# Norm 1 by column scale: chunks of a transposed input, and the tokens' inverse norms applied to the mixer's products

## The chip, the core and the metric

The kernel runs on one core of a Trainium2 chip. The core's engines work side by side, each through its own list of instructions: TensorE (PE, with its weight loads as PEld), VectorE (DVE), ScalarE (ACT), GpSimd (POOL), and SyncE (SP), which here issues nearly all DMAs. The metric is device time in microseconds of one execution.

## The reference, cut to what matters

```python
h = rms_norm(x, norm1)                   # x * rsqrt(mean(x*x) + EPS) * norm1, 2048 tokens of 1024
p = h @ w_in
lru_x, lru_g, q, k, v, g, z = split(p)
lru_x = causal_depthwise_conv(lru_x)     # then two gates and a scan over the sequence
lru_o = rg_lru(lru_x) * gelu(lru_g)
log_alpha = log_sigmoid(z @ gla_w_alpha + gla_b_alpha) / 16
o = gla_chunk_causal(q / 8, k, v, log_alpha)
gla_o = rms_norm(o, gla_norm) * silu(g)
x = x + concat(lru_o, gla_o) @ w_out
x = x + ffn(rms_norm(x, norm2))          # SwiGLU, 1024 -> 2 x 2816 -> 1024
return rms_norm(x, final_norm)
```

All is float32. The norm's inverse root is one number for each token, norm1 one for each column of `x`.

## The kernel before, in words

The 2048 tokens are worked in four blocks of 512 (`b` = 0 to 3), and in a block in four tiles of 128 (`t`). Each large product is three matmuls (`mm3`, L248 to L250): both operands are split into a high part (a cast on ACT) and a low part (a subtraction on DVE), which `split` does at L258 and `split_scaled` with a column scale at L283 and L284. A part of `h`, the normed input, is needed with its 128 columns on the partitions and the 512 tokens along the rows, and there are eight such chunks in a block.

`Norm1` makes them. It loads the block's four tiles of `x` (tokens on partitions), sums their squares on ACT (`sumsq`, L219), takes the inverse roots on DVE (`rsqrt`, eleven small instructions, L231 to L240, from `rv` to `rs`), scales the tiles on DVE (L310), and transposes them chunk by chunk on PE (L320 in the first block, L329 later).

`mixer(b)` then runs, on PE in this order: the products for k and z (L562 reads them), four products for the conv channels, each followed by the conv on ACT and DVE (`lru_conv`), the products for v with the eight gate products between them (`lru_gates`), two products for q (`feat(h)`, read at L641), the state updates (L654), the output half of the block before or, in block 0, `lru_out`, and so on. Behind the last gate stands a chain on two other engines: ACT takes a root (L622) and an exponential (L625), and DVE runs the four scans of the channel groups (`lru_scan`, L525 to L529; the scan itself is L527). In the program's text the next block's `Norm1` is made behind these scans, and its transposes are spread over `lru_out`.

The order of instructions on each engine is not that of the text: a scheduler sets it when the program is built, by its own estimate of times. What an engine has been given it works off in that order. Buffers in the arena are handed out by hand; a load into a reused place waits until the last reader is done, and everything behind it on SP waits too. PSUM has eight banks (`mm`).

Of the kernel before, what the change touches and what calls it, by code (L numbers as in the profile page):

```python
# [15 lines left out]
P = 128  # L16
# [162 lines left out]
def hybrid_layer_kernel(  # L179
    ctx: ExitStack,  # L180
    tc: tile.TileContext,
    x: bass.AP,
    wf: bass.AP,
    wkz: bass.AP,
    wv: bass.AP,
# [28 lines left out]
    def small(n, name):  # L214
        return cp.tile([P, n], F32, tag=f"s{n}", name=name, bufs=10 if n < 16 else 6)
# [81 lines left out]


    class Norm1:
        def __init__(self, b, group=TT):  # L300
            self.xs = [load(x_v[b * TT + t], D) for t in range(TT)]
            for g in range(0, TT, group):
                ss = small(group, "ss")
                for i in range(group):
                    sumsq(ss[:, i : i + 1], self.xs[g + i].f(D), D)
                rs = small(group, "rs")
                rsqrt(rs, [ss], 1.0 / D, group)
                for i in range(group):
                    v = self.xs[g + i].f(D)
                    nc.vector.tensor_scalar(v, v, rs[:, i : i + 1], None, op0=ALU.mult)  # L310
            self.h = []

        def half(self, g):
            if g == 0:
                self.h = [pair(T, True) for _ in range(KC)]
            for c in range(KC):
                ps = bank()
                for i in range(2):
                    v = self.xs[2 * g + i].f(D)
                    nc.tensor.transpose(ps[:, i * P : (i + 1) * P], v[:, c * P : (c + 1) * P], ident)  # L320
                split_scaled(self.h[c], ps[:, : 2 * P], cc(C_N1 + c), slice(2 * g * P, (2 * g + 2) * P))
            if g == 1:
                A.free(*self.xs)

        def chunk(self):
            c = len(self.h)
            ps = bank()
            for t in range(TT):
                nc.tensor.transpose(ps[:, t * P : (t + 1) * P], self.xs[t].f(D)[:, c * P : (c + 1) * P], ident)  # L329
            b = pair(T, True)  # L330
            split_scaled(b, ps, cc(C_N1 + c), slice(0, T))
            self.h.append(b)
            if c == KC - 1:
                A.free(*self.xs)


    class Feed:
# [53 lines left out]
    feed = Units(all_units, 2)  # L391

    wal_b, zta_b = A.alloc(256), A.alloc(T)
    nxt = Norm1(0, 2)
    nc.sync.dma_start(ident, ident_in)
    nc.sync.dma_start(col, cols)
    feed.ahead = 4
    feed.fill()
    feed.ahead = 2

    sfx = cp.tile([P, P], F32, name="sfx")
    nc.sync.dma_start(sfx, sfx_in)
# [71 lines left out]
    def tokmaj_first(norm, n):  # L474

        pss = [bank() for _ in range(TT)]
        wbs = [feed.get() for _ in range(4)]
        for g in range(2):
            norm.half(g)
            for c in range(KC):  # L480
                wh, wl = wbs[c // 2][c % 2].r(n)
                mh, ml = norm.h[c].r(T)
                for t in (2 * g, 2 * g + 1):
                    s = slice(t * P, (t + 1) * P)
                    mm3(pss[t][:, :n], mh[:, s], ml[:, s], wh, wl, c == 0, c == KC - 1)
        for wb in wbs:
            A.free(*wb)
        return pss

    def lru_conv(b, f, ps):  # L490
        buf = A.alloc(T)
        xc = buf.f(T)
        nc.scalar.activation(xc, ps, AF.Identity, scale=cc(C_CW + 12 + f), bias=cc(C_CB + f))
        hl = cp.tile([P, 3], F32, tag="halo", name="halo", bufs=8)
        nc.vector.tensor_copy(hl, ps[:, T - 3 : T])
        for s in (1, 2, 3):
            w = cc(C_CW + (3 - s) * 4 + f)
            nc.vector.scalar_tensor_tensor(xc[:, s:], ps[:, : T - s], w, xc[:, s:], op0=ALU.mult, op1=ALU.add)
            if b > 0:
                nc.vector.scalar_tensor_tensor(  # L500
                    xc[:, :s], halo[f][:, 3 - s : 3], w, xc[:, :s], op0=ALU.mult, op1=ALU.add
                )
        halo[f] = hl
        return buf

    def lru_gates(f, xcb):
# [47 lines left out]
    def mixer(b, norm, prev, side):  # L554
# [4 lines left out]
        pss = tokmaj_first(norm, 272) if b == 0 else tokmaj(norm.h, 272, [lambda: run(side, 1)] * 4)  # L559
        h = norm.h  # L560
        for t, ps in enumerate(pss):
            nc.scalar.copy(kz[:, t, :], ps[:, :272])  # L562
        xcs = [lru_conv(b, 0, feat(h))]
        run(side, 2)
        zps = bank()
        for t in range(TT):
            nc.tensor.transpose(zps[:16, t * P : (t + 1) * P], kz[:, t, 256:272], ident)
        nc.vector.tensor_copy(zta[:16, :], zps[:16, :])
        xcs.append(lru_conv(b, 1, feat(h)))
        run(side, 2)  # L570
        zfs = []
        for t2 in range(2):
# [13 lines left out]
                nc.scalar.activation(las[t2].f(), las[t2].f(), AF.Ln, bias=1.0)  # L586
        for t2 in range(2):
            nc.vector.scalar_tensor_tensor(las[t2].f(), zfs[t2], 0.0, las[t2].f(), op0=ALU.min, op1=ALU.subtract)
        xcs.append(lru_conv(b, 2, feat(h)))
        run(side)  # L590
        xcs.append(lru_conv(b, 3, feat(h)))
        dps = bank()
        dview = dps[:, :16].rearrange("p (a n) -> p a n", a=2)
        eks = []
# [29 lines left out]
            for f in range(4):  # L624
                nc.scalar.activation(gts[f][0].f(), gts[f][0].f(), AF.Exp, scale=sc_a[:, f : f + 1])  # L625
        vs = []
        for ps in vps:
            v = A.alloc(T)
            nc.scalar.copy(v.f(), ps)
            vs.append(v)  # L630
        hs = [lru_scan(b, f, gts[f]) for f in range(4)]
        after = None
        if b + 1 < NB:
            after = Norm1(b + 1)


        qs = []
        for a in range(2):
            ps = feat(h)
            q = A.alloc(T)  # L640
            nc.scalar.activation(q.f(), ps, AF.Copy, scale=0.125)  # L641
            qs.append(q)
        state = stc[(b + 1) % 2]
        sts = []
# [35 lines left out]
        def lru_out():  # L680
            for f in range(4):
                ps = feat(h)
                g = A.alloc(T)
                nc.scalar.activation(g.f(), ps, AF.Gelu_apprx_tanh)
                nc.vector.tensor_mul(g.f(), g.f(), hs[f].f())
                mixt[f] = split(g.f(), T)
                A.free(g, hs[f])
                if after is not None:
                    for _ in range((0, 2, 3, 3)[f] if b == 0 else 2):
                        after.chunk()  # L690
# [44 lines left out]

        for t, ps in enumerate(tokmaj(h, T)):
            sg = A.alloc(T)
            nc.scalar.activation(sg.f(), ps, AF.Silu)
# [8 lines left out]

        if b > 0:
            lru_out()
        A.free(*h)  # L750
        for hd in range(4):
            ps = bank()
            for t in range(TT):
# [627 lines left out]
def _layout(i):  # L1381
    import numpy as np

    f = {k: np.asarray(v) for k, v in i.items()}
    w_in = f["w_in"][0]
    c = np.ascontiguousarray

    def featu(w):
        k, m = w.shape
        return c(w.reshape(k // P, P, m // P, P).transpose(2, 1, 0, 3)).reshape(m // P, P, k)  # L1390

    def toku(w):
# [24 lines left out]
    ind = np.where(t[:, None] // 64 == np.arange(2)[None, :], 1.0 / 16.0, 0.0)  # L1417
    return {
        "x": c(f["x"][0]), "wf": wf, "wkz": wkz, "wv": wv, "wg": wg, "wo": wo, "wgu": wgu, "w2": w2,
        "cols": c(cols), "wgate": c(wgate), "walpha": c(walpha), "fnorm": c(f["final_norm"]),  # L1420
        "ident": np.eye(P, dtype=np.float32), "sfx": sfx.astype(np.float32), "ind": ind.astype(np.float32),
    }
# [19 lines left out]
```

## Time and profile before

| | |
|---|---|
| median of 3 runs | 2057.82 us (2056.31 to 2059.64) |
| profiled execution | 2056.9 us, of it span 2055.1 us |
| PE busy | 2004.1 us, 98% of the span |
| DVE, ACT busy | 1335.3 us (65%), 884.0 us (43%) |
| TensorE clock granted, mean | 0.991 |

The mixer blocks take about the first 750 us of the span, the feed-forward part the rest. A busy PE is one with a matmul under way, so the 51 us in which it is not busy are the waits that a change can take away, and what is shorter or gone in its matmuls comes beside them. A wait is read by its releaser: the instruction, on another engine, whose end let the waiting one start.

### The profile page before, as it was taken

How to read it: one execution, taken by the hardware profiler on the slowest of the kernel's cores; microseconds unless marked ns; L12 is line 12 of the kernel's file. 1: busy time of each engine (PE TensorE's matmuls, PEld its weight loads, DVE VectorE, ACT ScalarE, POOL GpSimd, SP SyncE). 2: the span in 40 equal slices, each digit the busy share in tenths (PEclk: the TensorE clock that was granted, in tenths of full speed). 3: DMA queues.
4: the chain of work that ended last, by engine and by line, in shares of the span. 5: the costliest groups of instructions: out<-in, count | busy, mean ns of one | idle time of the engine just before them, and what ended most of it. 6: DMA issues, size and time to landing. Idle time of an engine off the chain costs nothing.

```text
span 2055.1 us, 26677 instructions
## 1 busy us (share of the span) xinstructions
PE 2004.1 (98%) x9520; PEld 1652.2 (80%) x9520; DVE 1335.3 (65%) x2390; ACT 884.0 (43%) x1523; POOL 178.0 (9%) x216
## 2 busy tenths in 40 slices
PE   7999999999999999999999999999999999999997
PEld 6878788878878878888888887888888788888876
DVE  5575656575555586666777777777775555656676
ACT  5655635654553454443444554444443212212332
POOL 0000000000000000000011001111120222222110
PEclk9999999999999999999999999999999999999999
DMA  5142245243524653567467656577576955755642
GB/s 184 44 153 72 90 147 191 77 141 126 170 69 153 204 180 113 169 199 221 159 217 228 191 152 218 193 219 236 195 235 221 354 164 177 242 170 159 227 131 82
DMA packets 211174, 353.21 MB, mean 172 GB/s; under 512 B 19409, under 2 KB 95458, under 8 KB 211042
## 3 DMA queue, kind: packets, MB, share of 16 engines
q1 hardware_dynamic: 196898, 304.32, 46.1%
q0 software_dynamic: 14144, 47.20, 6.1%
q8 instruction: 74, 1.21, 0.3%
q14 instruction: 58, 0.48, 0.1%
HBM read 244.49 MB, written 106.95 MB: 171 GB/s over the span
## 4 chain that ended last, share of the span: by engine, by line
PE 89%; DVE 4%; ACT 2%; DMA 2%; issue 1%; POOL 0%; DVEq 0%; SPq 0%; POOLq 0%; ACTq 0%
PE mm L248 29%; PE mm L249 29%; PE mm L250 29%; DMA arena_r<-w2c 1%; DVE arena L527 1%; PE mm L858 1%; DMA arena_r<-ad 1%; DVE arena L525 0%; DVE arena L526 0%; PE mm L329 0%; ACT arena L622 0%; PE mm L600 0%; PE mm L710 0%; PE mm L576 0%; DVE arena_r L258 0%
## 5 line engine op out<-in xcount | busy, mean ns | idle before, releaser
L249 PE MATMUL mm<-arena_r 128*128 128x512 f32 (+1 forms) x2596 | 1004.6, 387 | 9.4 <-DVE carry L529 8.0
L250 PE MATMUL mm<-arena_r 128*128 128x512 f32 (+1 forms) x2584 | 998.3, 388 | 0.9 <-DVE arena_r L258 0.9
L248 PE MATMUL mm<-arena_r 128*128 128x512 f32 (+1 forms) x2512 | 980.2, 391 | 9.0 <-DVE arena L1199 8.0
L249 PEld LDWEIGHTS mm<-arena_r 128*128 128x128 f32 x2596 | 489.9, 189 | 104.7 <-DVE carry L529 8.9
L248 PEld LDWEIGHTS mm<-arena_r 128*128 128x128 f32 x2512 | 473.3, 189 | 121.8 <-DVE arena L1199 13.6
L250 PEld LDWEIGHTS mm<-arena_r 128*128 128x128 f32 x2584 | 487.9, 189 | 100.7 <-DVE arena_r L258 1.3
L258 ACT CAST arena_r<-arena 128x512 fp32r<-128x512 f32 (+1 forms) x465 | 277.3, 612 | 461.5 <-PE mm L249 241.2
L258 DVE TENSOR_TENSOR arena_r<-arena,arena_r 128x512 fp32r<-128x512 f32 (+1 forms) x464 | 308.9, 677 | 217.8 <-ACT arena_r L258 204.1
L1199 DVE TENSOR_TENSOR arena<-arena,mm 128x512 f32<-128x512 f32 x272 | 186.3, 686 | 142.6 <-PE mm L250 142.5
L1165 ACT CAST arena_r<-arena_r 128x896 fp32r<-128x896 f32 (+1 forms) x88 | 80.1, 915 | 288.2 <-PE mm L249 184.5
L1070 POOL DMA_DIRECT2D w2c<-arena x127 | 68.7, 541 | 770.8 <-DMA ad<-arena 376.8
L1166 POOL TENSOR_TENSOR arena_r<-arena_r 128x896 fp32r<-128x896 f32 x40 | 85.4, 2136 | 320.4 <-PE mm L250 125.9
L258 ACT CAST arena_r<-swing 128x512 fp32r<-128x512 f32 x90 | 55.8, 621 | 106.8 <-PE mm L249 37.3
L219 ACT ACTIVATE arena<-arena 128x512 bf16<-128x512 f32 (+1 forms) x64 | 46.9, 733 | 81.8 <-DVE arena L1199 26.0
L258 ACT CAST swing<-arena 128x512 fp32r<-128x512 f32 (+1 forms) x83 | 48.1, 593 | 70.2 <-PE mm L250 30.3
L258 DVE TENSOR_TENSOR arena_r<-swing,arena_r 128x512 fp32r<-128x512 f32 x90 | 61.7, 687 | 22.9 <-ACT arena_r L258 18.7
L249 PE MATMUL mm<-arena_r,swing 128*128 128x512 f32 x164 | 65.3, 398 | 4.2 <-DVE arena_r L258 4.2
L959 ACT COPY arena<-mm 128x512 f32<-128x512 f32 x100 | 58.4, 584 | 22.8 <-PE mm L250 21.9
L248 PE MATMUL mm<-swing,arena_r 128*128 128x512 f32 (+1 forms) x164 | 60.5, 369 | 3.8 <-DVE arena_r L284 2.2
L248 PE MATMUL mm<-arena_r,swing 128*128 128x512 f32 x156 | 62.5, 402 | 0.0
L982 DVE TENSOR_TENSOR arena<-mm,arena 128x512 f32<-128x512 f32 x43 | 29.7, 691 | 50.3 <-PE mm L250 50.3
L250 PE MATMUL mm<-swing,arena_r 128*128 128x512 f32 (+1 forms) x168 | 61.2, 365 | 0.0
(210 smaller groups left out, 1650.3 us busy)
## 6 DMA issues: line engine op xcount, KB each, us to landing
arena_r<-w2c SPq DMA_DIRECT2D x148, 256.0 KB, 5.3
arena<-in_wgu_dram SPq DMA_DIRECT2D x142, 256.0 KB, 3.8
arena_r<-ad SPq DMA_DIRECT2D x80, 448.0 KB, 3.5
w2c<-arena POOLq DMA_DIRECT2D x127, 256.0 KB, 3.6
ad<-arena SPq DMA_DIRECT2D x122, 256.0 KB, 3.2
arena<-in_wf_dram SPq DMA_DIRECT2D x40, 512.0 KB, 3.5
arena<-in_wo_dram SPq DMA_DIRECT2D x32, 512.0 KB, 3.9
arena<-in_w_dram SPq DMA_DIRECT2D x41, 256.0 KB, 4.4
```

What stands on the lines that cost most here:

```text
L219: nc.scalar.activation(b.ap.bitcast(BF16), src, AF.Square, accum_out=dst)
L248: nc.tensor.matmul(ps, lhsT=sh, rhs=mh, start=first, stop=False, skip_group_check=again)
L249: nc.tensor.matmul(ps, lhsT=sh, rhs=ml, start=False, stop=False, skip_group_check=again)
L250: nc.tensor.matmul(ps, lhsT=sl, rhs=mh, start=False, stop=last, skip_group_check=again)
L258: b.ins = [nc.scalar.copy(hi, src).ins, nc.vector.tensor_sub(lo, src, hi.bitcast(F32)).ins]
L527: nc.vector.tensor_tensor_scan(m, a, u, 0.0 if b == 0 else carry[f], op0=ALU.mult, op1=ALU.add)
L959: nc.scalar.copy(b.f(), ps[:, :n])
L982: nc.vector.tensor_mul(u1.f(), pa[:, :n], u1.f())
L1070: nc.gpsimd.dma_start(w2c[k][:, m, i * T : (i + 1) * T], part.f())
L1165: nc.scalar.copy(hi, v)
L1166: (nc.gpsimd if i == 1 else nc.vector).tensor_tensor(lo, v, hi.bitcast(F32), op=ALU.subtract)
L1199: nc.vector.tensor_add(c, c, ps)
```

## The change

`x` comes a second time, laid out as `xt` with columns on partitions, chunk by chunk. `Norm1.chunk` now loads a chunk of `xt` and splits it with the column scale norm1; there are no transposes and no scaled tiles. The split parts lack the tokens' inverse norms, so everything made from them is scaled afterwards: products with tokens on partitions by the column `rs` (in the ACT instruction that reads them: k and z, v, the silu gate), products with tokens along the rows by a tile `rb`, which holds the inverse norms along the row, alike on all partitions (on DVE: the conv's input, q, the gelu gate). `scales` makes both: it still loads the four tiles of `x`, sums squares and takes roots, then widens each of the four columns to 128 equal columns on DVE and multiplies them with the identity on PE, and ACT copies the bank to `rb`.

```diff
     class Norm1:
+        def __init__(self, b):
+            self.b = b
             self.h = []
+            self.raws = []
+        def fetch(self):
+            c = len(self.h) + len(self.raws)
+            if c < KC:
+                self.raws.append(load(xt[self.b, c], T))
         def chunk(self):
             c = len(self.h)
-            ps = bank()
-            for t in range(TT):
-                nc.tensor.transpose(ps[:, t * P : (t + 1) * P], self.xs[t].f(D)[:, c * P : (c + 1) * P], ident)
+            raw = self.raws.pop(0)
             b = pair(T, True)
-            split_scaled(b, ps, cc(C_N1 + c), slice(0, T))
+            split_scaled(b, raw.f(), cc(C_N1 + c), slice(0, T))
+            A.free(raw)
             self.h.append(b)
+            self.fetch()
+        def scales(self):
+            ss = small(TT, "ss")
+            xs = [load(x_v[self.b * TT + t], D) for t in range(TT)]
+            for t in range(TT):
+                sumsq(ss[:, t : t + 1], xs[t].f(D), D)
+            A.free(*xs)
+            self.rs = cp.tile([P, TT], F32, tag="rs1", name="rs1", bufs=2)
+            rsqrt(self.rs, [ss], 1.0 / D, TT)
+            wide = A.alloc(T)
+            ps = bank()
+            for t in range(TT):
+                w = wide.f(TT, P)[:, t, :]
+                nc.vector.tensor_copy(w, self.rs[:, t : t + 1].to_broadcast([P, P]))
+                nc.tensor.matmul(ps[:, t * P : (t + 1) * P], lhsT=w, rhs=ident, start=True, stop=True)
+            A.free(wide)
+            self.rb = A.alloc(T)
+            nc.scalar.copy(self.rb.f(), ps)
...
-    def lru_conv(b, f, ps):
+    def lru_conv(b, f, ps, rb):
+        raw = A.alloc(T)
+        nc.vector.tensor_mul(raw.f(), ps, rb)
+        ps = raw.f()
...
-            nc.scalar.copy(kz[:, t, :], ps[:, :272])
+            nc.scalar.activation(kz[:, t, :], ps[:, :272], AF.Copy, scale=norm.rs[:, t : t + 1])
...
             after = Norm1(b + 1)
+            after.fetch()
+            after.fetch()
+            after.scales()
...
-            nc.scalar.activation(q.f(), ps, AF.Copy, scale=0.125)
+            nc.vector.scalar_tensor_tensor(q.f(), ps, 0.125, rb, op0=ALU.mult, op1=ALU.mult)
...
-                nc.scalar.activation(g.f(), ps, AF.Gelu_apprx_tanh)
+                nc.vector.tensor_mul(g.f(), ps, rb)
+                nc.scalar.activation(g.f(), g.f(), AF.Gelu_apprx_tanh)
```

In block 0 the k and z products are no longer made in two halves of the tokens: `tokmaj_first` splits two chunks, multiplies them for all four tiles, and so on, and calls `scales` at its end. In the blocks behind it `scales` is called right behind the text of the scans, as above. What the scheduler makes of it shows in three places.

On PE in block 0, at the end of the v products: before, the last gate product (bank 763) is followed by the first product for q (bank 839).

```order
L248 MATMUL mm_763<-arena_r_64 128x512
L249 MATMUL mm_763<-arena_r_64 128x512
L250 MATMUL mm_763<-arena_r_64 128x512
L248 MATMUL mm_839<-arena_r_64 128x512
L249 MATMUL mm_839<-arena_r_64 128x512
```

Now, with the last gate product in bank 701 and q's first in bank 785, `scales` of block 1 (L336) stands between them.

```order
L249 MATMUL mm_701<-arena_r_64 128x512
L250 MATMUL mm_701<-arena_r_64 128x512
L251 MATMUL mm_701<-arena_r_64 128x512
L336 MATMUL mm_770<-ident_67,arena_63 128x128 x4
L249 MATMUL mm_785<-arena_r_64,swing_65 128x512
L250 MATMUL mm_785<-arena_r_64,swing_65 128x512
```

The four products of the inverse norms have been put in ahead of q and of the state updates; blocks 1 and 2 have them in the same place.

On DVE in block 0, around the four scans: before, two low parts of weights (L258) and the state updates' sums (L669) come behind the scans (L525 to L529), and only then the roots (`rv`).

```order
L525 SCALAR_TENSOR_TENSOR arena<-arena 128x512
L526 TENSOR_TENSOR arena<-arena 128x512 x2
L527 SCALAR_TENSOR_TENSOR arena<-arena 128x512 x2
L529 COPY carry<-arena 128x1
L258 TENSOR_TENSOR arena_r<-arena,arena_r 128x512
L529 COPY carry<-arena 128x1
L258 TENSOR_TENSOR arena_r<-arena,swing 128x512
L669 SCALAR_TENSOR_TENSOR arena<-stc_169,dec,mm 128x128 x2
L669 SCALAR_TENSOR_TENSOR arena<-arena,dec,mm 128x128 x5
L231 TENSOR_SCALAR rv<-ss 128x4
```

Now the scans (L540 to L544) are followed by three low parts of chunks (L285) and the roots; behind the piece shown come seven more of the small instructions and the four copies (L335) that the products at L336 take.

```order
L540 SCALAR_TENSOR_TENSOR arena<-arena 128x512
L541 TENSOR_TENSOR arena<-arena 128x512 x2
L542 SCALAR_TENSOR_TENSOR arena<-arena 128x512 x2
L544 COPY carry<-arena 128x1
L285 SCALAR_TENSOR_TENSOR arena_r<-arena,col,arena_r 128x512
L544 COPY carry<-arena 128x1
L285 SCALAR_TENSOR_TENSOR arena_r<-arena,col,arena_r 128x512 x2
L232 TENSOR_SCALAR rv<-ss 128x4
L236 TENSOR_SCALAR ry<-rv 128x4
L239 SCALAR_TENSOR_TENSOR rt<-ry 128x4
L240 TENSOR_TENSOR rt<-rt,rv 128x4
L259 TENSOR_TENSOR arena_r<-arena,arena_r 128x512
```

The roots have moved ahead of the state updates' sums, but stay behind all four scans.

On SP at the start: before, the four tiles of `x` are the first loads.

```order
L272 DMA arena<-in_x_dram 128x1024 x4
L395 DMA ident<-in_ident_dram 128x128
L396 DMA col<-in_cols_dram 128x49
L272 DMA arena<-in_wkz_dram 128x544 x4
L272 DMA arena<-in_wf_dram 128x1024
```

Now they are the 25th to 28th transfer. Ahead of the piece shown stand the column constants, three chunks of `xt` and two weights of the k and z products; the piece begins with the small constants.

```order
L408 DMA ident<-in_ident_dram 128x128
L411 DMA sfx<-in_sfx_dram 128x128
L413 DMA ind<-in_ind_dram 128x2
L415 DMA arena<-in_walpha_dram 17x256
L422 DMA arena<-in_wgate_dram 64x4x64 x4
L273 DMA arena<-in_xt_dram 128x512 x2
L273 DMA arena<-in_wkz_dram 128x544 x2
L273 DMA arena<-in_xt_dram 128x512 x2
L273 DMA arena<-in_wf_dram 128x1024
L273 DMA arena<-in_xt_dram 128x512
L273 DMA arena<-in_wf_dram 128x1024 x2
L273 DMA arena<-in_x_dram 128x1024 x4
```

The `x` tiles, on which only `scales` depends, have moved from the head of the queue to behind all chunks, all weights of k and z, and three of the conv's weights (`wf`).

## Rows read from the trace of the kernel before

**Rows 1.** The page: span, and busy time (share) and count of each engine.

```profile
span 2055.1 us, 26677 instructions
PE 2004.1 (98%) x9520; PEld 1652.2 (80%) x9520; DVE 1335.3 (65%) x2390; ACT 884.0 (43%) x1523; POOL 178.0 (9%) x216
```

**Rows 2.** PE's waits, whole span: releaser, us in total, times, longest.

```profile
PE mm L320 <- DVE arena L310: 9.8, 1, 9.8
PE mm L249 <- DVE carry L529: 8.0, 2, 4.1
...
PE mm L249 <- DVE arena_r L258: 5.6, 2, 4.2
...
PE mm L329 <- DVE arena L310: 1.0, 3, 0.3
```

**Rows 3.** Groups by form, 0 to 760 us: count | busy us, mean ns | idle before.

```profile
L329 PE MATMUL mm<-ident,arena 128*128 128x128 f32 x96 | 12.9, 274 | 1.4 <-DVE arena L310 1.0 <-PE mm L250 0.5
...
L545 DVE TENSOR_TENSOR arena<-arena,mm 128x512 f32<-128x512 f32 x32 | 20.2, 682 | 3.5 <-PE mm L250 3.5
...
L310 DVE TENSOR_SCALAR arena<-arena,rs 128x1024 f32<-128x1024 f32 x16 | 11.4, 768 | 0.1
```

**Rows 4.** The chain that ended last: start us, us, pieces (L576 has 256 columns).

```profile
45.29 1.92 PE mm L576 x8
...
122.91 1.31 PE mm L329 x12
```

**Rows 5.** Timeline of PE at five places: start us, us, instruction, idle before.

```profile
33.78 0.40 PE L248 MATMUL mm<-arena_r 128*128 128x512 f32 x1
...
88.93 0.39 PE L248 MATMUL mm<-arena_r 128*128 128x512 f32 x1
...
224.79 0.39 PE L248 MATMUL mm<-arena_r,swing 128*128 128x512 f32 x1
...
242.59 0.80 PE L249 MATMUL mm<-arena_r,swing 128*128 128x512 f32 x1 [4.20 <-DVE arena_r L258]
...
410.75 0.39 PE L248 MATMUL mm<-arena_r,swing 128*128 128x512 f32 x1
```

**Rows 6.** Timeline of DVE behind the gates of blocks 0, 1 and 2.

```profile
103.21 2.33 DVE L527 TENSOR_TENSOR_SCAN arena<-arena 128x512 f32<-128x512 f32 x2
...
109.35 0.17 DVE L231 TENSOR_SCALAR rv<-ss 128x4 f32<-128x4 f32 x1 [0.17 <-ACT arena L219]
...
232.15 1.29 DVE L525 SCALAR_TENSOR_TENSOR arena<-arena 128x512 f32<-128x512 f32 x2 [5.52 <-ACT arena L625]
...
239.44 2.46 DVE L527 TENSOR_TENSOR_SCAN arena<-arena,carry 128x512 f32<-128x512 f32 x2
...
249.88 0.17 DVE L231 TENSOR_SCALAR rv<-ss 128x4 f32<-128x4 f32 x1 [1.94 <-ACT arena L219]
250.09 0.17 DVE L235 TENSOR_SCALAR ry<-rv 128x4 int32<-128x4 int32 x1
...
425.34 2.46 DVE L527 TENSOR_TENSOR_SCAN arena<-arena,carry 128x512 f32<-128x512 f32 x2
...
435.45 0.17 DVE L231 TENSOR_SCALAR rv<-ss 128x4 f32<-128x4 f32 x1 [1.61 <-ACT arena L219]
```

**Rows 7.** Timeline of ACT in block 1: the first sum of squares.

```profile
244.46 1.06 ACT L219 ACTIVATE arena<-arena 128x1024 bf16<-128x1024 f32 x1 [8.54 <-DMA arena<-in_x_dram]
```

**Rows 8.** Loads of x, 0 to 130 us: from issue to landing.

```profile
DMA to landing us min/median/max: 3.5/4.9/6.2
```

**Rows 9.** Busy us by stretch: PE, PEld, DVE, ACT, POOL; PEclk, DMA share, GB/s.

```profile
4.00:12.00 8.00, 2.04 (x9) 1.65 (x10) 4.71 (x21) 7.05 (x16) 1.18 (x2) 1.00 1.04 403
...
242.00:249.00 7.00, 6.41 (x16) 5.05 (x17) 5.94 (x20) 4.23 (x8) 0.40 (x1) 0.53 0.87 304
...
300.00:350.00 50.00, 49.97 (x283) 43.53 (x282) 29.64 (x58) 24.76 (x48) 0.00 (x0) 1.00 0.52 171
...
429.50:433.00 3.50, 3.50 (x10) 2.71 (x9) 3.50 (x15) 1.33 (x3) 0.00 (x0) 0.51 0.94 365
```

More of the change, by code (lines that the diff above doesn't have):

```diff
@@ L182, in hybrid_layer_kernel @@
     x: bass.AP,
+    xt: bass.AP,
     wf: bass.AP,
@@ L299, in hybrid_layer_kernel @@
     class Norm1:
[L300 to L310, printed above, removed]
-            self.h = []
@@ L313, in half @@
[L313 to L316, printed above, removed]
-                ps = bank()
[L318 to L323, printed above, removed]
+        def __init__(self, b):
+            self.b = b
+            self.h = []
+            self.raws = []
@@ L325, in chunk @@
+        def fetch(self):
+            c = len(self.h) + len(self.raws)
+            if c < KC:
+                self.raws.append(load(xt[self.b, c], T))
         def chunk(self):
             c = len(self.h)
+            raw = self.raws.pop(0)
+            b = pair(T, True)
+            split_scaled(b, raw.f(), cc(C_N1 + c), slice(0, T))
+            A.free(raw)
+            self.h.append(b)
+            self.fetch()
[8 more added lines that the diff above has]
+            wide = A.alloc(T)
@@ L327, in chunk @@
             ps = bank()
             for t in range(TT):
-                nc.tensor.transpose(ps[:, t * P : (t + 1) * P], self.xs[t].f(D)[:, c * P : (c + 1) * P], ident)
-            b = pair(T, True)
-            split_scaled(b, ps, cc(C_N1 + c), slice(0, T))
-            self.h.append(b)
-            if c == KC - 1:
-                A.free(*self.xs)
+                w = wide.f(TT, P)[:, t, :]
+                nc.vector.tensor_copy(w, self.rs[:, t : t + 1].to_broadcast([P, P]))
+                nc.tensor.matmul(ps[:, t * P : (t + 1) * P], lhsT=w, rhs=ident, start=True, stop=True)
@@ L393, in hybrid_layer_kernel @@
     wal_b, zta_b = A.alloc(256), A.alloc(T)
-    nxt = Norm1(0, 2)
-    nc.sync.dma_start(ident, ident_in)
     nc.sync.dma_start(col, cols)
-    feed.ahead = 4
+    nxt = Norm1(0)
+    nxt.fetch()
+    feed.fetch()
+    nxt.fetch()
+    nxt.fetch()
+    feed.ahead = 1
     feed.fill()
     feed.ahead = 2
+    nc.sync.dma_start(ident, ident_in)
     sfx = cp.tile([P, P], F32, name="sfx")
@@ L476, in tokmaj_first @@
         pss = [bank() for _ in range(TT)]
[L477 to L481, printed above, removed]
+        for kp in range(4):
+            for _ in range(2):
+                norm.chunk()
+            wb = feed.get()
+            for i in range(2):
+                wh, wl = wb[i].r(n)
+                c = 2 * kp + i
                 mh, ml = norm.h[c].r(T)
-                for t in (2 * g, 2 * g + 1):
+                for t in range(TT):
                     s = slice(t * P, (t + 1) * P)
                     mm3(pss[t][:, :n], mh[:, s], ml[:, s], wh, wl, c == 0, c == KC - 1)
-        for wb in wbs:
             A.free(*wb)
+        norm.scales()
         return pss
-    def lru_conv(b, f, ps):
+    def lru_conv(b, f, ps, rb):
+        raw = A.alloc(T)
+        nc.vector.tensor_mul(raw.f(), ps, rb)
+        ps = raw.f()
         buf = A.alloc(T)
@@ L503, in lru_conv @@
         halo[f] = hl
+        A.free(raw)
         return buf
@@ L561, in mixer @@
         for t, ps in enumerate(pss):
-            nc.scalar.copy(kz[:, t, :], ps[:, :272])
-        xcs = [lru_conv(b, 0, feat(h))]
+            nc.scalar.activation(kz[:, t, :], ps[:, :272], AF.Copy, scale=norm.rs[:, t : t + 1])
+        rb = norm.rb.f()
+        xcs = [lru_conv(b, 0, feat(h), rb)]
         run(side, 2)
@@ L568, in mixer @@
         nc.vector.tensor_copy(zta[:16, :], zps[:16, :])
-        xcs.append(lru_conv(b, 1, feat(h)))
+        xcs.append(lru_conv(b, 1, feat(h), rb))
         run(side, 2)
@@ L588, in mixer @@
             nc.vector.scalar_tensor_tensor(las[t2].f(), zfs[t2], 0.0, las[t2].f(), op0=ALU.min, op1=ALU.subtract)
-        xcs.append(lru_conv(b, 2, feat(h)))
+        xcs.append(lru_conv(b, 2, feat(h), rb))
         run(side)
-        xcs.append(lru_conv(b, 3, feat(h)))
+        xcs.append(lru_conv(b, 3, feat(h), rb))
         dps = bank()
@@ L626, in mixer @@
         vs = []
-        for ps in vps:
+        for t, ps in enumerate(vps):
             v = A.alloc(T)
-            nc.scalar.copy(v.f(), ps)
+            nc.scalar.activation(v.f(), ps, AF.Copy, scale=norm.rs[:, t : t + 1])
             vs.append(v)
@@ L737, in mixer @@
             sg = A.alloc(T)
-            nc.scalar.activation(sg.f(), ps, AF.Silu)
+            nc.scalar.activation(sg.f(), ps, AF.Silu, scale=norm.rs[:, t : t + 1])
             sgv = sg.f(2, 2, P)
@@ L749, in mixer @@
             lru_out()
-        A.free(*h)
+        A.free(*h, norm.rb)
         for hd in range(4):
@@ L1418, in _layout @@
     return {
-        "x": c(f["x"][0]), "wf": wf, "wkz": wkz, "wv": wv, "wg": wg, "wo": wo, "wgu": wgu, "w2": w2,
+        "x": c(f["x"][0]), "xt": c(f["x"][0].reshape(NB, T, KC, P).transpose(0, 2, 3, 1)), "wf": wf, "wkz": wkz, "wv": wv, "wg": wg, "wo": wo, "wgu": wgu, "w2": w2,
         "cols": c(cols), "wgate": c(wgate), "walpha": c(walpha), "fnorm": c(f["final_norm"]),
```

## The prediction

> **What bounds the kernel now.** I read the page first: PE is busy for 2004.1 of 2055.1 us [rows 1], so the time is PE's work plus about 51 us of waits. The list of PE's waits says where they are [rows 2]: 9.8 us at the start, until the first tiles of x are scaled, and waits of some 4 us each in the blocks. The timeline of PE places the one of block 1 at 242.59, 4.20 us [rows 5]. The timeline of DVE shows why: the scans run until 241.90 (239.44 + 2.46), and the low part of a weight stands behind them [rows 6]. So the scans are already the place where PE runs out of work: behind the last gate DVE first idles 5.52 us for ACT's root and exponential, then starts the scans at 232.15 [rows 6]. Before, PE had something to do in that time: q's products from 224.79 on [rows 5] and the state updates. The reader should keep this gap in mind, because the change puts something into it.
>
> **The transposes that go.** In blocks 1 to 3, 96 transposes (L329) take 12.9 us at most, with the overlap to their neighbours counted in [rows 3]. Twelve in a row take 1.31 us in the chain, 0.109 each [rows 4]: 96 x 0.109 = 10.5 us. I take the chain's value, since matmuls overlap; 12.9 is the other end. Their three short waits for L310 go too, 1.0 us [rows 2].
>
> The Trainium skill (TensorE: Matmul & The Clock Gate, Part 4: PE-mode transpose) gives about 275 ns for a 128x128 transpose inside a kernel. The row's mean of one, 274 ns [rows 3], looks the same, but the chain shows that they follow each other at 0.109 us. By the page 26.4 us would be saved and the sum below would be 15.9 us less.
>
> **The products that come.** Each `scales` adds four f32 products of 128 columns. The trace has none; the nearest row is L576, f32 with 256 columns, where four products are eight records in 1.92 us, 0.24 a record [rows 4]. At half the columns 0.12, so 12 products for blocks 1 to 3 are 24 x 0.12 = 2.9 us (between 1.9 and 5.8: a fixed cost as large as the whole, or none). The four of block 0 are in the start below.
>
> **The wait that comes.** In blocks 0, 1 and 2 the order on PE now has these products between the last gate and q's first product. They need the copies L335, which need the roots, which stand in DVE's order behind all four scans. PE works its list in order (through the 4.20 us before 242.59 nothing that stands behind the waiting matmul was started [rows 5]), so q, the state updates and all behind them wait. How long is read from the same places before. q's first product began at 88.93, 224.79 and 410.75 [rows 5]; that is when PE will now arrive at L336. The last scan ended at 105.54, 241.90 and 427.80 [rows 6], 16.6, 17.1 and 17.1 us later. The first step of the roots (`rv`) came at 109.35, 249.88 and 435.45 [rows 6], since it needs the squares of all four tiles, and these come late: ACT idled 8.54 us for the load of the first one [rows 7], and the tiles' places in the arena come free only as the scans end. From q's place to `rv` it is 20.4, 25.1 and 24.7 us, together 70.2. I take these three, block by block, because loads, sums and scans keep their order; the lower end is `rv` at the end of the scans (50.8 in all), the upper end adds one load of 4 us in each block, where the longest load takes 6.2 us [rows 8] (82).
>
> From `rv` on it is eleven dependent small instructions at 0.21 us (249.88 to 250.09 [rows 6]), 2.3 us, and four copies of 128 columns, between the 0.17 us of a 4-column instruction [rows 6] and the 0.68 of one with 512 columns [rows 3]; I take 0.25 each, 1.0 us. That is 3.3 in each block, and 0.7 more in block 0, where a low part stands among them: 10.6. New waits: 70.2 + 10.6 = 80.8 us.
>
> What is taken away again: the waits of 4.2 and 4.1 us in blocks 1 and 2 [rows 2, 5], since DVE is far ahead when PE resumes; with the 1.0 of the transposes 9.3 us. The wait of block 3 stays: it has no `scales`. Net 71.5 us.
>
> **The clock.** Behind its waits of 4 us PE was granted 0.53 of its clock over 242 to 249 and 0.51 over 429.5 to 433 [rows 9], that is the lower of its two levels, 1.2 instead of 2.4 GHz: 7 x 0.47 = 3.3 and 3.5 x 0.49 = 1.7 us of work lost. Blocks 1 and 2 pay that already. Block 0 gets it new, and so does the start: 2.5 us each. Nothing in the rows speaks for more after a longer wait; if each cost 3.3, it would be some 3 us in all.
>
> **The start.** PE will begin earlier, since a chunk and a weight come in 0.5 MB instead of x in 2 MB. But `scales` of block 0 stands on PE right behind the k and z products, and the fourth tile of x is now the 28th transfer. Up to it there are 8 chunks of 256 KB, 4 weights of 272, 3 of 512, 4 tiles of 512 and 0.5 MB of constants: 7.3 MB, at 403 GB/s [rows 9] 18 us. With 2 us for the first landing and 3 for the stops of the queue (estimates: loads reuse places and wait for splits) it lands at 23. One square sum 1.25, `rv` to the copies 3.3, a low part 0.7 and the four products 0.5 make it 29, where the first conv product began at 33.78 [rows 5]. So 4.8 us are won and 2.5 lost to the clock: -2.3. Ends: without any stop -6; with the tile at 29, as late as a load of 6.2 us behind two stops would make it, +4.
>
> **What is hidden.** On DVE each block gets ten multiplications of 512 columns (0.68 us, as L545 [rows 3]) and four copies, and loses four scalings at 0.77 [rows 3]: about 5 us in 180. DVE is busy 30 of 50 us beside a full PE [rows 9], which covers it; uncovered, the conv's multiplication would cost PE 0.7 us at each of 16 places, 11 us. 8.4 MB more are loaded, beside queues that are half busy [rows 9]. The scales on ACT ride in instructions that are there anyway.
>
> **The sum**, against the profiled execution: 2056.9 + 71.5 - 10.5 + 2.9 + 2.5 - 2.3 = 2121.0 us. That execution lies 0.9 us below the median of the runs, so I predict **2122 us**, 3.1% slower.
>
> **Rivals.**
>
> *Squares ready in time (chance 0.15).* The order of loads has changed with the arena: two of the next block's tiles could be in place long before, and `rv` then follows the scans at once. New waits 50.8 + 10.6; the sum falls by 19 to 2102. The 1.94 us that DVE waits for ACT even at `rv` [rows 6] speaks against it.
>
> *Loads one after another (0.12).* Each reused place starts its load only when a scan has ended, and a chunk's split on ACT stands among the sums of squares and waits for its own load. 82 instead of 70.2: 2133, with a late start 2138.
>
> *Hidden, not slower than before (0.04, of it 0.01 by so little that it can't be told).* If the roots were ready when PE arrives, only the work counts: 2056.9 - 10.5 + 2.9 - 1.0 - 2.3 = 2046, 2047 against the median. It decides in favour of the change only if the three new waits stay below about 20 us together, under 7 each. Against it: even the start of the scans comes 7.4 us after q's place (224.79 to 232.15 [rows 5, 6]), and the scans alone take almost 10. It would need the roots ahead of the scans on DVE, and the order shows them behind.
>
> The forecast itself has 0.69. Range: 2099 to 2140: it takes in the early squares (but not together with an early start) and the late loads with the late start; some 0.1 lie below or above. Differences under 0.2%, about 4 us, can't be told from no change: faster by more 0.03, within 0.01, slower by more 0.96.
>
> **What would show it.** In the profile after: PE's longest waits are at L336, for the copies L335, four of them: three of 23 to 29 us behind the gates, and one of 6 to 9 us before 30 us. The two waits of 4 us behind the state updates in blocks 1 and 2 are gone, one is left. PE's busy time falls by some 10 us net of slow stretches. The first conv product starts near 29 us. I would be wrong if the list of waits had no long L336, if they ended before the scans, or if PE's list were worked out of order.

## The result and the profile after

The changed kernel takes 2120.41 us (median of 4 runs, 2116.92 to 2124.41) where the kernel before took 2058.23: a ratio of 1.0306, with a 95% interval of 1.0293 to 1.0319 (the two medians alone give 1.0302). It is 3.1% slower, and 2122 was predicted. The profiled span grew from 2055.1 to 2115.1 us; the profiled execution is the fastest of the four. One execution of a later run (E9) took 5165.52 us, for a reason that its record does not show, and is left out of that run's ratio.

The page of the changed kernel, to be set beside [rows 1]:

```profile
span 2115.1 us, 26513 instructions
PE 1996.0 (94%) x9424; PEld 1644.8 (78%) x9424; DVE 1357.6 (64%) x2411; ACT 894.7 (42%) x1513; POOL 179.4 (8%) x216
```

PE works 8.1 us less and the span is 60.0 us longer, so PE waits 68.1 us more. Its list of waits up to 760 us, which answers to [rows 2] (releaser, us in total, times, longest):

```profile
PE mm L336 <- issue: 64.0, 3, 27.5
PE mm L336 <- DVE arena L335: 22.8, 1, 22.8
PE mm L250 <- DVE arena_r L259: 6.3, 2, 4.2
PE mm L249 <- ACT swing L259: 5.4, 1, 5.4
PE mm L878 <- DVE arena L873: 1.2, 2, 1.0
```

Four waits at L336, the products of the inverse norms, make 86.8 us. For three of them the list names no instruction ("issue"); what they waited for is read from the timelines. First PE, at these four places and at the first conv product (start, us, instruction, idle before), answering to [rows 5]:

```profile
30.04 2.05 PE L336 MATMUL mm<-ident,arena 128*128 128x128 f32 x8 [9.51 <-issue]
31.74 0.77 PE L249 MATMUL mm<-arena_r 128*128 128x512 f32 x1
...
116.31 2.05 PE L336 MATMUL mm<-ident,arena 128*128 128x128 f32 x8 [27.54 <-issue]
...
270.10 2.08 PE L336 MATMUL mm<-ident,arena 128*128 128x128 f32 x8 [22.76 <-DVE arena L335]
...
476.51 2.04 PE L336 MATMUL mm<-ident,arena 128*128 128x128 f32 x8 [27.00 <-issue]
```

Then DVE at the three places in blocks 0, 1 and 2, answering to [rows 6]: the last scans (L542), the roots' first step (`rv`), and in block 0 the copies (L335).

```profile
102.88 2.33 DVE L542 TENSOR_TENSOR_SCAN arena<-arena 128x512 f32<-128x512 f32 x2
...
113.30 0.17 DVE L232 TENSOR_SCALAR rv<-ss 128x4 f32<-128x4 f32 x1 [0.29 <-ACT arena L220]
...
115.98 0.63 DVE L335 COPY arena<-rs 128x128 f32<-128x128 f32 x4
...
261.84 2.46 DVE L542 TENSOR_TENSOR_SCAN arena<-arena,carry 128x512 f32<-128x512 f32 x2
...
267.64 0.17 DVE L232 TENSOR_SCALAR rv<-ss 128x4 f32<-128x4 f32 x1 [1.31 <-ACT arena L220]
...
464.01 2.46 DVE L542 TENSOR_TENSOR_SCAN arena<-arena,carry 128x512 f32<-128x512 f32 x2
...
474.00 0.17 DVE L232 TENSOR_SCALAR rv<-ss 128x4 f32<-128x4 f32 x1 [0.29 <-ACT arena L220]
```

Each wait can be cut into three. In block 0 PE arrives at 88.77 (116.31 - 27.54); the scans end at 105.21, 16.4 us later; `rv` starts 8.1 us after that; the first product follows 3.0 us after `rv`. In block 1 the three pieces are 17.0, 3.3 and 2.5 us, in block 2 17.0, 7.5 and 2.5.

Why `rv` is late in block 0 shows on ACT's timeline, answering to [rows 7]:

```profile
101.99 0.72 ACT L284 ACTIVATE arena_r<-arena,col 128x512 fp32r<-128x512 f32 x1 [3.91 <-DMA arena<-in_xt_dram]
...
105.10 1.06 ACT L220 ACTIVATE arena<-arena 128x1024 bf16<-128x1024 f32 x1 [0.55 <-DMA arena<-in_x_dram]
...
108.89 1.06 ACT L220 ACTIVATE arena<-arena 128x1024 bf16<-128x1024 f32 x1 [1.47 <-DMA arena<-in_x_dram]
...
111.50 0.72 ACT L284 ACTIVATE arena_r<-arena,col 128x512 fp32r<-128x512 f32 x1 [1.46 <-DMA arena<-in_xt_dram]
112.13 1.04 ACT L220 ACTIVATE arena<-arena 128x1024 bf16<-128x1024 f32 x1
```

In block 0 the squares begin as the scans end and wait for their loads, and the last one stands behind a chunk's split (L284) that waits for a load of its own. Last, the clock, by stretches around the waits of blocks 0 and 1 and behind that of block 2 (columns as in [rows 9]):

```profile
93.00:116.00 23.00, 0.00 (x0) 0.00 (x0) 14.05 (x32) 12.74 (x21) 0.00 (x0) 0.51 0.40 126
116.00:124.00 8.00, 7.69 (x29) 6.64 (x30) 1.31 (x5) 1.21 (x2) 0.00 (x0) 0.71 0.16 66
250.00:270.00 20.00, 0.00 (x0) 0.00 (x0) 13.77 (x32) 13.02 (x22) 0.00 (x0) 0.51 0.36 122
270.00:278.00 8.00, 7.90 (x30) 6.74 (x31) 1.14 (x5) 1.21 (x2) 0.00 (x0) 0.74 0.07 26
476.00:490.00 14.00, 13.49 (x51) 11.32 (x52) 3.36 (x9) 2.35 (x4) 0.00 (x0) 0.77 0.08 32
```

The lower of the clock's two levels (1.2 GHz) was granted while PE idled, and PE resumes at it: 8 x 0.29 = 2.3 us lost behind the first wait, 8 x 0.26 = 2.1 behind the second, 14 x 0.23 = 3.2 behind the third.

### The profile page after: what moved, and what is told of

Its sections match the earlier page's. It is cut to its first block, busy times and chain, and to the rows that moved or that the text cites. A ratio compares the mean times of both kernels' runs of the same rounds, so it can differ in the third digit from the quotient of the medians.

```text
span 2115.1 us, 26513 instructions
## 1 busy us (share of the span) xinstructions
PE 1996.0 (94%) x9424; PEld 1644.8 (78%) x9424; DVE 1357.6 (64%) x2411; ACT 894.7 (42%) x1513; POOL 179.4 (8%) x216
## 3 DMA queue, kind: packets, MB, share of 16 engines
HBM read 252.88 MB, written 106.95 MB: 170 GB/s over the span
## 4 chain that ended last, share of the span: by engine, by line
PE 88%; DVE 4%; ACT 3%; DMA 2%; issue 2%; POOL 0%; POOLq 0%; SPq 0%; DVEq 0%; ACTq 0%
PE mm L249 29%; PE mm L250 28%; PE mm L251 28%; DMA arena_r<-w2c 1%; DMA arena<-x2d 1%; PE mm L878 1%; DVE arena L542 1%; DVE arena L1219 1%; ACT arena L220 0%; DVE arena L540 0%; ACT arena L638 0%; DVE arena L541 0%; PE mm L336 0%; DMA arena<-in_xt_dram 0%; PE mm L730 0%
## 5 line engine op out<-in xcount | busy, mean ns | idle before, releaser
L250 PE MATMUL mm<-arena_r 128*128 128x512 f32 (+1 forms) x2712 | 1047.9, 387 | 4.5 <-DVE arena_r L259 4.5
L249 PE MATMUL mm<-arena_r 128*128 128x512 f32 (+1 forms) x2667 | 1037.4, 390 | 9.1 <-DVE arena L1219 8.6
L251 PE MATMUL mm<-arena_r 128*128 128x512 f32 (+1 forms) x2715 | 1043.8, 386 | 0.0
L249 PEld LDWEIGHTS mm<-arena_r 128*128 128x128 f32 x2667 | 502.8, 189 | 128.4 <-DVE arena L1219 14.9
L251 PEld LDWEIGHTS mm<-arena_r 128*128 128x128 f32 x2715 | 511.9, 189 | 103.5
L250 PEld LDWEIGHTS mm<-arena_r 128*128 128x128 f32 x2712 | 511.6, 189 | 103.5 <-DVE arena_r L259 5.8
L259 ACT CAST arena_r<-arena 128x512 fp32r<-128x512 f32 (+1 forms) x515 | 305.1, 608 | 554.6 <-PE mm L250 247.7
L259 DVE TENSOR_TENSOR arena_r<-arena,arena_r 128x512 fp32r<-128x512 f32 (+1 forms) x509 | 336.5, 675 | 273.4 <-ACT arena_r L259 226.7
L336 PE MATMUL mm<-ident,arena 128*128 128x128 f32 x32 | 8.2, 438 | 86.8 <-issue 64.0
L336 PEld LDWEIGHTS mm<-ident,arena 128*128 128x128 f32 x32 | 7.1, 328 | 88.2 <-issue 65.0
L1186 DVE TENSOR_TENSOR arena_r<-arena_r 128x896 fp32r<-128x896 f32 (+1 forms) x48 | 49.3, 1026 | 11.3 <-ACT arena_r L1185 11.2
L1002 DVE TENSOR_TENSOR arena<-mm,arena 128x512 f32<-128x512 f32 x41 | 28.3, 691 | 43.1 <-PE mm L251 43.1
L994 DVE TENSOR_TENSOR arena<-mm,arena 128x512 f32<-128x512 f32 x41 | 28.3, 690 | 35.9 <-PE mm L251 35.9
```

The lines of the kernel that those rows point to most:

```text
L249: nc.tensor.matmul(ps, lhsT=sh, rhs=mh, start=first, stop=False, skip_group_check=again)
L250: nc.tensor.matmul(ps, lhsT=sh, rhs=ml, start=False, stop=False, skip_group_check=again)
L251: nc.tensor.matmul(ps, lhsT=sl, rhs=mh, start=False, stop=last, skip_group_check=again)
L259: b.ins = [nc.scalar.copy(hi, src).ins, nc.vector.tensor_sub(lo, src, hi.bitcast(F32)).ins]
L994: nc.vector.tensor_add(u1.f(), pb[:, :n], u1.f())
L1002: nc.vector.tensor_mul(u1.f(), pa[:, :n], u1.f())
```

## The experiments

The theory: PE works its list in order (from 88.77 to 116.31 it started nothing, though in the kernel before q's first product ran at 88.93), the products stand in it ahead of q, and their operands come from instructions that stand behind the scans on DVE. The main rival: the added work on DVE, ACT and the queues is what costs, and the products only show it.

**E1, the products late.** `scales` is cut in two; loads, squares and roots stay, and the copies, the products and the bank's copy (`row`) go to the end of the block.

```diff
             rsqrt(self.rs, [ss], 1.0 / D, TT)
+
+        def row(self):
             wide = A.alloc(T)
...
         if b > 0:
             lru_out()
+        if after is not None:
+            after.row()
         A.free(*h, norm.rb)
```

> The changed kernel, but the four products of the next block's inverse norms (with the copies before and the bank's copy behind them) stand at the end of the block on PE; loads, squares and roots stay where they were. In-order wait at the products: their waits of 27.5, 22.8 and 27.0 us (77.3) go, the waits of 4.2 and 4.1 us that the kernel before had behind the state updates come back (+8.3), and 7.0 us of half clock behind the long waits become 4.7 (-2.3): 2120.4 - 77.3 + 8.3 - 2.3 = 2049 us, between 2044 and 2055, below the kernel before. Rival, the added work (ten multiplications a block on DVE, 8.4 MB of loads) is what costs, and the products only show it: the waits move to another instruction and the time stays at 2100 to 2121.

Measured: 2065.26 us, 1.0039 of the kernel before (1.0024 to 1.0054). PE's waits up to 760 us:

```profile
PE mm L250 <- DVE arena_r L259: 15.0, 5, 4.2
PE mm L249 <- ACT arena_r L259: 9.9, 3, 5.7
PE mm L338 <- issue: 9.8, 1, 9.8
```

The three long waits are gone (L338 is the product; only the wait at the start is left), and with them 55 us. That speaks for the theory. But the time is 16 us above the expected 2049: besides the waits of 4.2 us in blocks 1 to 3, new ones stand at parts of weights, the longest 5.7 us in block 0, behind the scans. So something in the change does cost more than the price of its instructions on PE, once the long waits are gone.

**E2, the products alone, in the kernel before.** The counterpart: nothing of the change but the copies, four products and the bank's copy, called right behind `Norm1(b + 1)`.

```diff
             after = Norm1(b + 1)
+            after.row()
```

> The kernel before, with only the four copies, the four products and the bank's copy added behind the roots of the next block; the result of the products is not used. PE has them between the last gate product and q's first product. In-order wait: three waits of 24 to 28 us appear at them, the waits of 4.2 and 4.1 us go, products and clock add 3 to 6: 2058 + 80.8 - 9.3 + 5.4 = 2135 us, between 2122 and 2142. Rival, the added work of the change is what costs: four small products for a block add at most 3 us, 2061.

Measured: 2124.59 us, 1.0327 (1.0312 to 1.0343). Its list of PE's waits begins:

```profile
PE mm L320 <- DVE arena L319: 77.4, 3, 26.9
```

Four small products a block, whose result nobody uses, make the kernel before as slow as the whole change did (the two intervals overlap). The waits of 4.2 and 4.1 us [rows 2] are gone from its list, as expected.

**E3, the roots early.** The x tiles of the next block are loaded, squared and their roots taken ahead of the v products; copies and products stay.

```diff
+        after = None
+        if b + 1 < NB:
+            after = Norm1(b + 1)
+            after.scales()
         gts = []
...
-            after.scales()
+            after.row()
```

> The changed kernel, but the x tiles of the next block are loaded, squared and their roots taken ahead of the v products, so that the roots stand ahead of the scans on DVE; the copies still stand behind the scans and the products in their place on PE. In-order wait: of each wait the part up to the scans' end stays, 105.1 - 88.8 = 16.4 us in block 0, and about 1 for the copies; three waits of 17 to 18.5 instead of 27.5, 22.8 and 27.0, 24 us less: 2096, between 2090 and 2102. Rival, late loads set the wait alone: with the loads early all of it goes, 2049. Rival, added work: no change, 2120.

Measured: 2100.48 us, 1.0215 (1.0196 to 1.0234). The products on PE in blocks 0, 1 and 2:

```profile
105.19 1.19 PE L338 MATMUL mm<-ident,arena 128*128 128x128 f32 x4 [17.00 <-issue]
...
254.17 1.22 PE L338 MATMUL mm<-ident,arena 128*128 128x128 f32 x4 [17.20 <-DVE arena L337]
...
453.76 1.65 PE L338 MATMUL mm<-ident,arena 128*128 128x128 f32 x6 [17.19 <-DVE arena L337]
```

What stays of each wait is the part up to the scans' end, 17.0 to 17.2 us; what is gone are the late squares and the roots. The wait is cut where the theory cuts it.

**E4, the copies early too.** The copies are made right behind the early roots, so that only the products are left at the old place (the edit is shown against E3).

```diff
-        def row(self):
-            wide = A.alloc(T)
+            wide = self.wide = A.alloc(T)
...
+        def row(self):
+            wide = self.wide
             ps = bank()
```

> As the kernel with early roots, but the four copies are made right behind the roots, ahead of the scans; the products stay in their place on PE between the last gate product and q's first product. In-order wait: the operands are there when PE arrives, no wait of over 3 us at the products, the waits of some 4 us behind the state updates are back: 2049 us as with late products, between 2044 and 2057. Rival, the place on PE itself costs: over 2075. Rival, added work: over 2100.

Measured: 2069.00 us, 1.0053 (1.0037 to 1.0070). The products in the blocks wait for nothing (L341 has one wait left, at the start), though PE has them where the changed kernel has them: the place brings no wait once the operands are there. But the time missed 2049 by 20 us. The list of waits, timelines of ACT and PE in block 2 and the clock show why (L622 is the product of the cumulated decays with the constant sfx; L603, L605 and L608 are an absolute value, an exponential and a logarithm on ACT, for each half of the block):

```profile
PE mm L622 <- DVE arena L610: 12.3, 2, 6.7
PE mm L341 <- issue: 8.9, 1, 8.9
```

```profile
363.00 1.28 ACT L608 ACT_TABLE_LOAD   x1
364.29 0.63 ACT L608 ACTIVATE arena<-arena 128x512 f32<-128x512 f32 x1
...
371.79 0.60 ACT L603 ACTIVATE arena<-mm 128x512 f32<-128x512 f32 x1 [4.09 <-DMA xq0b<-arena]
...
375.43 1.28 ACT L608 ACT_TABLE_LOAD   x1
```

```profile
378.13 1.22 PE L622 MATMUL mm<-arena,sfx 128*128 128x256 f32 x2 [6.71 <-DVE arena L610]
```

```profile
378.00:390.00 12.00, 11.87 (x39) 10.18 (x40) 5.37 (x14) 4.72 (x8) 0.00 (x0) 0.57 0.52 173
570.00:584.00 14.00, 13.22 (x41) 11.16 (x42) 5.61 (x14) 4.10 (x6) 0.00 (x0) 0.54 0.23 72
```

The second half's chain starts 4.09 us late, released by a store out of the arena, and it runs by itself: the logarithm's table is loaded at 363.00 for the first half and again at 375.43 for the second. PE waits 6.7 us for the end of it, and 5.6 in block 3; behind these waits the lower clock costs some 5.1 and 6.1 us more (0.43 of 11.87 and 0.46 of 13.22 us busy). In the changed kernel the two halves went through together in block 2 and PE waited for nothing there.

**E5, the start.** In block 0 PE gets the first two conv products ahead of the inverse norms.

```diff
+        first = [feat(h)]
+        if b == 0:
+            first.append(feat(h))
+            norm.row()
-        xcs = [lru_conv(b, 0, feat(h), rb)]
+        xcs = [lru_conv(b, 0, first.pop(0), rb)]
```

> The changed kernel, but in block 0 the products of the inverse norms stand behind the first two conv products on PE instead of ahead of them; all blocks behind as in the changed kernel. In-order wait: two conv products are 11 us of work, which fill the 9.5 us from the last k and z product (20.5) to the products at 30.0; with some 1.8 us of half clock behind that wait 11 us less: 2109, between 2106 and 2113. Rival, the start is bound by loads and splits of the conv's weights: the wait moves to them and less than 4 us are won, 2117 to 2121.

Measured: 2130.84 us, 1.0368 (1.0352 to 1.0384): 10 us slower than the changed kernel, where 11 less were expected. The start itself did what was expected of it, by half: the wait of 9.5 us became 1.0 and one of 2.9 for z, and z's transposes came at 33.85 where the changed kernel has them at 38.94. It was lost later, as in E4 (waits, then the clock behind the two at L622):

```profile
PE mm L338 <- DVE arena L337: 74.8, 3, 26.0
PE mm L622 <- DVE arena L610: 11.3, 2, 6.1
```

```profile
420.00:432.00 12.00, 10.56 (x36) 9.14 (x37) 5.36 (x13) 4.13 (x7) 0.00 (x0) 0.57 0.13 44
634.00:650.00 16.00, 13.19 (x42) 11.15 (x43) 6.36 (x15) 6.09 (x9) 0.00 (x0) 0.57 0.20 67
```

Little of the loss is waiting: up to 760 us all of PE's waits make 102.0 us, against 99.7 in the changed kernel. What grew is PE's busy time, from 1996.0 to 2011.2 us in the profiled executions (this one is the slowest of its four). Of these 15 us some 10 are the lower clock in the two stretches shown, an estimate (0.43 of 10.56 and 13.19 us busy).

**E6, late products and the new start.** E1 and E5 together.

> Late products in blocks 0 to 2 and the changed start in block 0 together. In-order wait: the two gains add, 2049 - 11 = 2038 us, between 2032 and 2045, 1% below the kernel before. If the start is bound by its loads: 2046 to 2049.

Measured: 2070.00 us, 1.0067 (1.0054 to 1.0079). The gains did not add. PE's list has a wait of 7.4 us for weight parts in block 0 and one of 5.7 at L622 in block 3: the start's 6 us are given back at the places where the other engines are late.

**E7, the transposes' price.** In the kernel before each of the 96 transposes is made twice.

```diff
-            for t in range(TT):
+            for t in (*range(TT), *range(TT)):
                 nc.tensor.transpose(...)
```

> The kernel before, with each of the 96 transposes of blocks 1 to 3 made twice into the same place; the result is the same. At the chain's spacing of 0.109 us 96 more cost 10.5 us: 2068.7, between 2067 and 2072. At the 0.274 us that the row gives as the mean of one they cost 26.3: 2084.5. If PE's time there is hidden behind other waits: 2058.

Measured: 2067.67 us against 2056.16 beside it, 1.0050 (1.0037 to 1.0063): 11.5 us by the medians and 10.3 by the ratio, 0.11 to 0.12 for one; the interval makes it 8 to 13 us. The group of them:

```profile
L329 PE MATMUL mm<-ident,arena 128*128 128x128 f32 x192 | 23.4, 273 | 1.8 <-DVE arena L310 1.0 <-PE mm L250 0.8
```

The mean of one is still 273 ns, since matmuls overlap; the price is near the spacing in the chain (0.109). The Trainium skill (TensorE: Matmul & The Clock Gate, Part 4: PE-mode transpose) gives about 275 ns, which is close to that mean; taken as the price it gives, as an estimate, 26 us more for this run. The measurement decides against that.

**E8, without the conv's multiplication.** E1, but the conv's input is not multiplied by the inverse norms; its later steps then read the bank itself, as in the kernel before.

```diff
-        nc.vector.tensor_mul(raw.f(), ps, rb)
-        ps = raw.f()
```

> The kernel with late products, but the conv's input is not multiplied by the inverse norms: 16 multiplications of 512 columns on DVE are left out. If DVE's added work is covered by PE: the time of the kernel with late products within 3 us (2049). If it is uncovered: 0.7 us at each of 16 places less, 11 us, 2038.

Measured: 2060.33 us, 1.0015 (1.0007 to 1.0024), against 1.0039 for E1: about 5 us of the possible 11, with intervals that just touch. DVE's added work is neither covered nor uncovered as a whole; without the long waits part of it shows in this order.

**E9, the decays later.** To test the reading of E4: E4, with the products of the decays (`decays` holds their text unchanged) behind the first quarter of the v products.

```diff
-        vps = tokmaj(h, T, [lambda f=f: gts.append(lru_gates(f, xcs[f])) for f in range(4)])
+        vps = tokmaj(h, T, [lambda f=f: (decays() if f == 0 else None, gts.append(lru_gates(f, xcs[f]))) for f in range(4)])
```

> As the kernel with early copies, but the products of the cumulated decays (with sfx and ind) stand in the v products, behind their first quarter, some 5.5 us of PE's work later. If the waits at them in blocks 2 and 3 (6.7 and 5.6 us), with some 3.5 us of half clock behind each, are what kept that kernel above the one before: 2069.0 - 12.3 - 7 = 2050, between 2045 and 2057, faster than before. Rival, DVE and ACT are behind there as a whole: the wait goes to the gates or the conv, 2063 to 2070.

Measured: 2047.20 us, 0.9954 (0.9941 to 0.9967). The waits at the decays are gone, and 21.8 us with them, where E4's waits and the lower clock behind them make 12.3 + 5.1 + 6.1 = 23.5: the kernel is faster than the one before. But the edit did more than move the products. In blocks 2 and 3 the two halves on ACT run together again, with one load for both logarithms (block 2):

```profile
368.09 1.28 ACT L608 ACT_TABLE_LOAD   x1
369.39 1.16 ACT L608 ACTIVATE arena<-arena 128x512 f32<-128x512 f32 x2
```

They end at 370.55, and the products start at 378.33. So E9 confirms what the waits cost; whether the later place or the joined halves removed them is not shown.

**E10, and the new start.** E9 with the start of E5.

> As the run with later decays, with the start that has the first two conv products ahead of the inverse norms in block 0, which had put block 0's state updates 5 to 6 us earlier: 2050 - 5 = 2045, between 2038 and 2052, 0.6% faster than before. Rival, DVE is behind as a whole: 2058 to 2068.

Measured: 2041.75 us, 0.9926 (0.9913 to 0.9939). This is the fastest of all, 0.7% under the kernel before and 3.7% under the changed one. Its page, and PE's longest waits up to 760 us:

```profile
span 2044.0 us, 26501 instructions
PE 1996.1 (98%) x9424; PEld 1643.0 (80%) x9424; DVE 1355.9 (66%) x2411; ACT 890.0 (44%) x1511; POOL 181.8 (9%) x216
```

```profile
PE mm L250 <- DVE arena_r L259: 8.0, 3, 4.2
PE mm L249 <- ACT swing L259: 5.2, 1, 5.2
PE mm L250 <- DVE carry L549: 3.6, 1, 3.6
...
PE mm L341 <- issue: 0.6, 1, 0.6
```

It does the changed kernel's arithmetic; the order alone differs. PE's busy time is the same (1996.1 against 1996.0), and the 71.1 us of span are waits. It also has all of the added loads (252.88 MB read in both) and the added work on DVE, so the main rival is ruled out as the cause of the 62 us.

**E11, the decays later in the kernel before.** The control for E9.

> The kernel before, with the products of the cumulated decays moved in the same way. It has no wait at them: no change, 2056 within 4 us. If the move itself were what wins, as much as in the others: 2040 to 2050.

Measured: 2056.09 us, 0.9997 (0.9989 to 1.0006): no change. The move by itself wins nothing where there is no wait at the decays.

## Why the prediction was right, step by step

**The place and the cause.** Right, and shown from both sides: the products alone bring the waits into the kernel before (E2), and with their operands ready the same place brings no wait (E4).

**The size of the waits.** Predicted 80.8 us, measured 27.5 + 22.8 + 27.0 = 77.3. From PE's arrival to `rv` 70.2 were read from the rows of before, and 24.5 + 20.3 + 24.5 = 69.3 came. That the sum agrees is in part luck: block 0 was 4.1 us longer than taken over, block 1 4.8 shorter. That loads, sums and scans keep their order held only roughly. The floor of 50.8 for the scans was 50.4, and E3 left 51.4. Behind `rv` 8.0 us instead of 10.6: the first product starts before the four copies are done (116.31, copies until 116.61), and the four take 0.63 us, not 1.0.

**What goes.** The two waits of 4.2 and 4.1 us are gone, the one of block 3 is there with 4.2, and the three short ones at the transposes are gone. In block 3 one of 2.1 us is new and was not foreseen.

**Transposes and products.** 96 transposes at 10.5 us; E7 gives 10.3 to 11.5 for as many more. The products at 0.12 a record: in E10, where three of the four groups follow no wait, eight records take 0.81 us from the first to the product behind them (81.30 to 82.11), 0.10 each, and that product takes 0.09 us longer than the ones behind it. In the changed kernel they are the first work behind a wait, at the lower clock, and the 32 take 8.2 us.

**The clock.** Predicted 2.5 us more in the blocks. Behind the three waits 2.3 + 2.1 + 3.2 = 7.6 are lost, where the kernel before lost 3.3 + 1.7 [rows 9]: 2.6 more. That block 0 would get it new was right.

**The start** is the term that was off. Predicted -2.3: 4.8 won, with the first conv product at 29, and 2.5 lost to the clock. It came at 31.74, so 2.0 were won, and z's transposes show what was left of the gain (kernel before, then after):

```profile
39.24 0.60 PE L567 MATMUL mm<-ident,arena 128*16 128x128 f32 x4
```

```profile
38.94 0.60 PE L583 MATMUL mm<-ident,arena 128*16 128x128 f32 x4
```

So -0.3: from the first conv product it is 5.5 us before and 7.2 after, 1.7 lost. Two terms were off. The prediction took one square sum behind the last tile, at 23 to 24.25; on ACT all four run from 21.43 to 26.99, one behind the other, and the products start at 30.04 instead of 28.5. And at the lower clock they take 1.7 us to the first conv product, not 0.5. That the start gets the lower clock new was misread: the kernel before was granted 0.54 over 16 to 23 us.

**What is hidden.** Right for this kernel, by its timeline: outside L336 PE waits 12.9 us up to 760. Wrong as a general statement: in the order of E1 about 5 us of the conv's multiplication show (E8). That the long waits were the cover in the changed kernel is a reading, not shown apart.

**The sum** by the measured terms, with the products as predicted: 77.3 - 9.3 - 11.5 + 2.9 + 2.6 - 0.3 + 2.1 = 63.8 us, against 64.1 predicted, 60.0 in the spans and 62.2 in the medians. Of the 3.8 to the spans, 0.9 is a wait of before at 106 us that is gone, with 0.5 each at two transposes; the rest lies in small differences that were not followed up.

**Rivals.** That the squares come in time is ruled out by `rv`, 8.1, 3.3 and 7.5 us behind the scans. Loads one after another were half true, in the ACT rows of block 0, and did not lengthen the sum (by the prediction's own terms the case with the late start is 2140, not 2138). E4 is the hidden case, made by an edit; 2047 was written for it, and it took E9's edit to come there (2047.2).

**Still open:** why E1 stays above the kernel before. Its PE is busy for 1996.3 us, 7.8 less than before, but waits 65.2 instead of 51.0, 9.9 of it for parts of weights; what makes these late is not shown. E8 puts about 5 us on the conv's multiplication; q's reading, which moved from ACT to DVE, and the roots among the state updates were not tried apart.

## What to carry to other kernels

A small product that needs a late operand costs the whole wait, since all that stands behind it in its engine's list is held up too; ask where the operand's last writer stands in its own engine's list, and what is ahead of it there. Here the order of work alone, with the same arithmetic, lies between 2131 us (E5) and 2042 (E10). After a long wait is removed, look at the waits again before judging: others come out, and the same edit (the new start) lost 10 us in one order and won 5 in another.

## What the runs showed that was not expected

The two halves of one ACT chain, run apart instead of together, cost two more table loads of 1.28 us each in a block (block 2 of E4 has four loads for them, the changed kernel two). The Trainium skill (ScalarE: Activation LUTs, Table sets: the hidden batching unit) has a set with both exponential and logarithm, by which neither order would load between them; here a load of 1.28 us stands each time that L608 follows L605.

PE was granted 0.51 of its clock while it stood still in the long waits, and what was lost behind a wait did not go by its length: 2.1 to 3.2 us behind 23 to 27 us, 3.3 behind 4.2 in the kernel before [rows 9], and 5.1 and 6.1 behind the 6.7 and 5.6 of E4, where PE first made the short products of the decays (378.13 to 384.98 in block 2).
